# Attention on one core: TensorE's order written out by hand, and q's rotation moved from GpSimd to VectorE

## The chip, the cores and the metric

The kernel runs on one core of a Trainium2 chip. A core has five engines, each with an instruction queue of its own: TensorE (PE in the profile; its weight loads are listed apart as PEld), VectorE (DVE), ScalarE (ACT), GpSimd (POOL) and SyncE (SP). They wait for each other by semaphores; DMA transfers are started from such a queue, in this kernel mostly from SP's and POOL's. The metric is the device time of one execution in microseconds, as the median over several runs; lower is better. The profile is one execution of the program recorded by the hardware profiler.

## The reference

Two layers of a diffusion transformer on 256 tokens of width 2048, with 256 context tokens beside them, in float32. Layer 0 mixes by a Fourier transform; layer 1, where the change lies, is windowed attention with 64 query heads of width 64, which share 8 key and value heads, with a sink per head. Cut to what matters:

```python
def _attend_with_sink(q, k, v, sink, mask=None):
    s = jnp.einsum('bqhgd,bkhd->bhgqk', q, k).astype(jnp.float32) * (ATTN_HEAD_DIM ** -0.5)
    if mask is not None:
        s = jnp.where(mask, s, NEG_INF)
    sk = jnp.broadcast_to(sink.astype(jnp.float32)[None, :, :, None, None], s.shape[:-1] + (1,))
    p = jax.nn.softmax(jnp.concatenate([s, sk], axis=-1), axis=-1)[..., :-1]
    return jnp.einsum('bhgqk,bkhd->bqhgd', p.astype(v.dtype), v)

def _attention_branch(h, hc, w_in, sink, rows, cols, need_ctx):
    q, k, v, z = jnp.split(h @ w_in, [D_BRANCH, D_BRANCH + kvw, D_BRANCH + 2 * kvw], axis=-1)
    kc, vc = jnp.split(hc @ w_in[:, D_BRANCH:D_BRANCH + 2 * kvw], 2, axis=-1)
    ...
    q = _axial_rope(q.reshape(b, n, ATTN_Q_HEADS, ATTN_HEAD_DIM), rows, cols)
    k = _axial_rope(k.reshape(b, n, ATTN_KV_HEADS, ATTN_HEAD_DIM), rows, cols)
    ...
    o = lax.map(block, ...)
    y = jnp.moveaxis(o, 0, 1).reshape(b, n, D_BRANCH) * jax.nn.silu(z)
```

Behind it stands `x + gate * (y @ w_out[1])` and a last RMS norm. `_axial_rope` is the rotary step: the 64 features of each head are multiplied by a table of cosines, and their swapped quarters by a table of sines, and the two are added.

## The kernel before

All is one function, `tile_dit`, on a framework that takes the instructions in program order, orders those of each engine anew by a timeline that it estimates itself when the program is built, and sets the semaphores. The order on each engine is fixed from then on: an instruction that waits holds up all behind it on its engine. `tc.issue_after(ins)` adds an edge that keeps the instructions in its block behind `ins` on the same engine; it costs no instruction.

Precision: a float32 operand is split into a high and a low half (`split`, L65: a cast on ACT at L66, a subtraction on DVE at L67), and a product is three matmuls (`mm3`, L144: L145, L146, L147). `half_split` makes the two weight tiles (`wh`, `wl`) of 1024 columns for one unit; the pool has six such buffers, three units.

The attention stage interleaves two kinds of work on PE:

- *Filler units.* `units` (L1400) lists them in order: eight units for each group of 512 columns of q ("q", one group for each of the 8 key heads `hk`), two for each of the 32 blocks of the gate z ("z"), and 14 of the first part of the output projection ("o"). The list goes: q0, q1, four z blocks, q2, four z blocks, and so on; "o" units end it. `emit_unit` (L1434) emits the next one and prepares the weights of the one behind it. The last unit of a q group calls `finish_q` (L1359); the last of a z block makes the gate (L1474, L1475).
- *Pairs of heads.* There are 32 (`b`), four for each `hk`. `stage_s` (L1491) makes a pair's scores: 12 matmuls at L1504 into four PSUM banks; then masking and row minimum on DVE (L1507), the exponential on ACT (L1511), normalisation with a split into two float16 halves (L1526 on ACT, L1527 on DVE), and, for all but the last pair, four DMA transposes on SP's queue (L1529). `stage_o` (L1532) makes the value product of 24 matmuls at L1538 into one bank, and `emit_y` (L1481) multiplies it by the gate on DVE (L1487). Pair 31 is transposed on PE (`pe_turn`, L1394) just ahead of its value product.

The loop at L1562 emits for each `b`: scores of pair `b`, two filler units, the value product of pair `b - 1`, two filler units. Ten units are emitted before the loop (L1543). What PE really does in which order is the framework's choice.

`finish_q` takes a finished q group from its two PSUM banks (`oq`, one for each block of 128 tokens). For `hk` 0, ACT takes the sum of squares (L1365) and DVE makes the rotary step straight from PSUM. For the other seven, ACT copies the bank to SBUF (L1369), takes the sum of squares (L1370), and POOL makes the rotary step from the copy. `roped` (L1129) is the step: one multiplication of 512 columns (L1132), two of 256 (L1137) and one addition of 512 (L1138), on the engine that it is given; without one it is DVE. Then four small operations on DVE turn the sum of squares into a scale (L1376 to L1379), and the scaling and split into float16 (`q_parts`: L1387 on ACT, L1388 on DVE) are deferred by some slots; the result `qt` is transposed on PE for `hk` 0 (L1397, with copies at L1398) and by DMA on SP's queue for the others (L1390). `prep_kk` (L1348) splits the keys of the group on ACT (L1354) and POOL (L1356).

PSUM has 8 banks, all of one pool: four for a pair's scores, one for a value product, two for a q group, one for a z block.

Of the kernel before, what the change touches and what calls it, by code (L numbers as in the profile page):

```python
# [13 lines left out]
AF = mybir.ActivationFunctionType  # L14
# [3 lines left out]
P = 128  # L18
D = 2048
KT = D // P  # L20
DB = 4096
NB = DB // P
N = 256
# [9 lines left out]
def tile_dit(ctx: ExitStack, tc: tile.TileContext, a: dict, out: bass.AP):  # L33
    nc = tc.nc
    V, S, PE, GP = nc.vector, nc.scalar, nc.tensor, nc.gpsimd
# [4 lines left out]
    actp = ctx.enter_context(tc.tile_pool(name="act", bufs=33))  # L40
# [14 lines left out]
    def act(dt=F32):  # L55
        return actp.tile([P, 512], dt, tag="act", name="act")
# [87 lines left out]
    def mm3(o, wh, wl, xh, xl, start, stop):  # L144
        PE.matmul(o, wh, xh, start=start, stop=False)  # L145
        PE.matmul(o, wh, xl, start=False, stop=False)  # L146
        return PE.matmul(o, wl, xh, start=False, stop=stop).ins  # L147
# [491 lines left out]
    for g in range(G):  # L639
        for j in {13: (8, 9), 14: (10, 11)}.get(g, (g - 5,) if 5 <= g < 13 else ()):  # L640
            t = up.tile([P, 1024], F32, name="pz", tag="pz", bufs=1)
# [13 lines left out]
        if g == 3:  # L655
            with tc.issue_after(f0_end[0]):
                f3 = [fold_uh(load_uh(g, kh), g, kh) for kh in range(2)]
            w = [split_uh(*f3[0]), {"m": split_part("m", f3[1][1])}]
# [3 lines left out]
        elif g == 4:  # L662
            w = []
# [476 lines left out]
    with tc.tile_pool(name="h1", reuse_waits="tile", bufs=16) as h1p:  # L1140
# [130 lines left out]
        with tc.tile_pool(name="at", reuse_waits="tile", bufs=2) as at:  # L1271
# [55 lines left out]
            def o1_step(k, os_, wh, wl):  # L1327
                while len(yh) <= min(k + 4, NB - 1) and (len(yh) < 28 or fin):
                    y_split(len(yh))
                for tb in range(2):  # L1330
                    mm3(os_[tb], yh[k][:, tb * P : (tb + 1) * P], yh[k][:, N + tb * P : N + (tb + 1) * P], wh, wl, k == 0, k == NB - 1)
            slot = [0]

            def k_turn(hp):
# [24 lines left out]
            def finish_q(hk, oq):  # L1359
                sq = at.tile([P, 2, 4], F32, tag="sq", name="sq")  # L1360
                qr = []
                for tb in range(2):
                    t = act()
                    if hk == 0:
                        S.activation(act(), oq[tb], AF.Square, accum_out=sq[:, tb, 0:1])  # L1365
                        roped(t, oq[tb], tb, actp, "act")
                    else:
                        t0 = act()
                        S.copy(t0, oq[tb])  # L1369
                        S.activation(act(), oq[tb], AF.Square, accum_out=sq[:, tb, 0:1])  # L1370
                        roped(t, t0, tb, actp, "act", GP)
                    qr.append(t)
                if hk:
                    prep_kk(hk)
                x, up, sc = (sq[:, :, c] for c in (1, 2, 3))
                V.tensor_scalar(x, sq[:, :, 0], 2.0**-70, None, op0=ALU.max)  # L1376
                V.tensor_scalar(x.bitcast(I32), x.bitcast(I32), 24, 23, op0=ALU.logical_shift_right, op1=ALU.logical_shift_left)
                V.tensor_scalar(up.bitcast(I32), x.bitcast(I32), -1.0, 204.0 * 2**23, op0=ALU.mult, op1=ALU.add)
                V.tensor_scalar(sc.bitcast(I32), x.bitcast(I32), kx.bitcast(I32), -30.0 * 2**23 - 2.0**31, op0=ALU.add, op1=ALU.add)  # L1379
                qt = at.tile([P, 8, 2, P], F16, tag="qt", name="qt")  # L1380
                qq[hk] = qt, sc
                for tb in range(2):
                    defer.append((slot[0], lambda tb=tb: q_parts(hk, tb, qt, qr[tb], up[:, tb : tb + 1])))
# [10 lines left out]
            def pe_turn(ft, f, tb):  # L1394
                o = pp.tile([P, 8, P], F16, tag="ps", name="ps")
                for j in range(8):
                    PE.transpose(o[:, j, :], f[:, j * P : (j + 1) * P], ident16)  # L1397
                (S.copy if tb == 0 else V.tensor_copy)(ft[:, :, tb, :], o)  # L1398
# [31 lines left out]
                return half_split(raws1[src], i % 2)  # L1430

            ready = {}

            def emit_unit():  # L1434
                if pos[0] >= len(ulist):
                    return
                u = ulist[pos[0]]
                if pos[0] not in ready:
                    ready[pos[0]] = prep(u)
                if pos[0] + 1 < len(ulist):  # L1440
                    ready[pos[0] + 1] = prep(ulist[pos[0] + 1])
                w = ready.pop(pos[0])
                pos[0] += 1
                kind, n, i, o = u
                if kind == "o":
                    if n == 0:
                        oA.extend([psum(), psum()])
                    for j in range(2):
                        o1_step(n * 2 + j, oA, *(t[:, j * 512 : (j + 1) * 512] for t in w))
                    return  # L1450
                wh, wl = w
                if kind == "q":
                    if i == 0:
                        o += [psum(), psum()]
                    if (n, i) == (0, 4):
                        with tc.issue_after(last_cast[0]):
                            prep_kk(0)
                    for j in range(2):
                        k = i * 2 + j
                        q = slice(j * 512, (j + 1) * 512)  # L1460
                        for tb in range(2):
                            mm3(o[tb], hx1[k][:, tb * P : (tb + 1) * P], hx1[k][:, N + tb * P : N + (tb + 1) * P], wh[:, q], wl[:, q], k == 0, k == KT - 1)
                    if i == 7:
                        finish_q(n, o)
                else:
                    if i == 0:
                        o.append(psum())
                    for k in range(i * 8, i * 8 + 8):
                        q = slice((k % 8) * P, (k % 8 + 1) * P)
                        mm3(o[0][:, 0:N], wh[:, q], wl[:, q], hx1[k][:, 0:N], hx1[k][:, N : 2 * N], k == 0, k == KT - 1)  # L1470
                    if i == 1:
                        th = at.tile([P, N], F32, tag="th", name="th", bufs=3)
                        zs = o[0][:, 0:N]
                        S.activation(th, zs, AF.Tanh, scale=0.5)  # L1474
                        V.scalar_tensor_tensor(th, th, 1.0, zs, op0=ALU.add, op1=ALU.mult)  # L1475
                        szs[n] = th
                        emit_y(n)
# [13 lines left out]
            def stage_s(b):  # L1491
# [6 lines left out]
                for tb in range(2):  # L1498
                    for hh in range(2):
                        so[hh, tb] = psum()  # L1500
                    for n, (jj, kx_) in enumerate(((j, kkh), (4 + j, kkh), (j, kkl))):
                        for hh in range(2):
                            r = slice(hh * 64, hh * 64 + 64)
                            PE.matmul(so[hh, tb], qt[r, jj, tb, :], kx_[r, :], start=n == 0, stop=n == 2)  # L1504
                    for hh in range(2):
                        o = so[hh, tb]
                        V.tensor_tensor_reduce(o, o, mask[:, tb, :], sc[:, tb : tb + 1], nsink[:, 2 * b + hh : 2 * b + hh + 1], ALU.add, ALU.min, mx[:, hh, tb : tb + 1])  # L1507
# [24 lines left out]
            def stage_o(blk, pair):  # L1532
                hk = blk // 4
                oo = psum()[:, 0:N]
                steps = [(kb, c, j) for kb in range(4) for c, j in ((0, kb), (64, kb), (0, 4 + kb))]
                for n, (kb, c, j) in enumerate(steps):
                    for hh, ft in enumerate(pair):
                        PE.matmul(oo[hh * 64 : hh * 64 + 64, :], v01[kb][:, hk, c : c + 64], ft[:, j, :, :].rearrange("p t q -> p (t q)"), start=n == 0, stop=n == len(steps) - 1)  # L1538
                obs[blk, 1] = oo
                emit_y(blk)  # L1540

# [9 lines left out]
            while defer:  # L1551
                defer.pop(0)[1]()

            def filler():
                j = slot[0]
                slot[0] += 1
                emit_unit()
                if defer and defer[0][0] + 2 < j:
                    defer.pop(0)[1]()

            pts = {}
            for b in range(33):  # L1562
                if b % 4 == 0:
                    while defer:
                        defer.pop(0)[1]()
                y_sums(12, 2 * b if b < 30 else 99)
                if b == 31:
                    out_scale()
                if b < 32:
                    pts[b] = stage_s(b)  # L1570
                filler()
                filler()
                if b:
                    ft, fs = pts.pop(b - 1)
                    for (hh, tb), f in fs.items():
                        pe_turn(ft[hh], f, tb)
                    stage_o(b - 1, ft)
                filler()
                filler()


        with tc.tile_pool(name="fin", reuse_waits="tile", bufs=1) as fp:
# [243 lines left out]
```

## Time and profile before

| | us |
|---|---|
| median of three runs | 1780.81 (1779.39 to 1782.48) |
| the profiled execution | 1778.66 |
| its span, first to last instruction | 1776.9 |
| PE busy in the span | 1717.7 |
| DVE busy in the span | 1385.8 |
| ACT busy in the span | 1112.8 |
| POOL busy in the span | 342.2 |

The attention stage's pairs run from about 1132 us (first scores) to 1637 us (last value product) of the span. A row of an order-of-time view gives start and length in microseconds, engine, line, operation, what is written from what, shapes and how many instructions the row merges; in square brackets stands the idle time of the engine just before it and what ended it. A row of the waits gives engine, tile and line that waited, what for, the total in microseconds, how often, and the longest. A matmul's recorded length overlaps that of the next; the distance between starts is what it costs. PE is counted busy by these overlapping lengths.

### The profile page before, as it was taken

What the parts mean: (1) busy time and instruction counts of PE and PEld (TensorE: products, weight loads), DVE (VectorE), ACT (ScalarE), POOL (GpSimd) and SP (SyncE); (2) the same over time, 40 slices, a digit from 0 to 9 for tenths busy, and PEclk for the clock granted to TensorE, in tenths of its full rate; (3) what the DMA queues carried; (4) which work ended last, traced back from release to release, by engine and by line L of the source; (5) the groups of instructions that cost most, each with busy time, mean ns of one, the idle gap of its engine ahead of it and who ended that gap; (6) DMA issues with size and microseconds to landing.
All of it is one profiled execution on the core that took longest, in us unless ns stands there. A gap on an engine that the chain in (4) does not pass through costs nothing. (4 is left out here: it accounts for less than half of the span.)

```text
span 1776.9 us, 28302 instructions
## 1 busy us (share of the span) xinstructions
PE 1717.7 (97%) x10379; PEld 1134.2 (64%) x10379; DVE 1385.8 (78%) x2334; ACT 1112.8 (63%) x2125; POOL 342.2 (19%) x485
## 2 busy tenths in 40 slices
PE   6999999999999999999999999699999999999998
PEld 4679999544444444446445646588777777877464
DVE  5779888797777796877687786878888889887755
ACT  5545556477768745465235696666677777786643
POOL 0002111212222115112311122202202220251001
PEclk9999999999999999999999999899999999999999
DMA  9998998778998969976997692588798788888643
GB/s 394 417 354 254 277 274 244 301 286 315 327 308 313 318 224 368 357 285 261 378 339 222 213 351 104 166 199 197 211 243 207 201 223 231 201 209 289 222 177 119
DMA packets 249196, 469.95 MB, mean 264 GB/s; under 512 B 171392, under 2 KB 171792, under 8 KB 222176
## 3 DMA queue, kind: packets, MB, share of 16 engines
q1 hardware_dynamic: 197568, 335.60, 57.9%
q0 software_dynamic: 47344, 125.58, 22.2%
q10 hardware_dynamic: 4144, 6.95, 1.1%
q8 instruction: 81, 1.33, 0.3%
q14 instruction: 59, 0.48, 0.1%
HBM read 419.30 MB, written 12.59 MB: 243 GB/s over the span
## 5 line engine op out<-in xcount | busy, mean ns | idle before, releaser
L67 DVE TENSOR_TENSOR wl<-raw,wh 128x1024 fp32r<-128x1024 f32 x152 | 191.5, 1270 | 101.8 <-ACT wh L66 85.8
L66 ACT CAST wh<-raw 128x1024 fp32r<-128x1024 f32 x152 | 158.1, 1046 | 81.7 <-PE ps L146 61.8
L146 PE MATMUL ps<-act,wf 128*128 128x512 f16 x512 | 194.0, 379 | 0.0
L147 PE MATMUL ps<-act,wf 128*128 128x512 f16 x512 | 191.1, 379 | 0.0
L145 PE MATMUL ps<-act,wf 128*128 128x512 f16 x512 | 189.8, 379 | 0.6 <-ACT wf L137 0.2
L145 PE MATMUL ps<-y,wf 128*128 128x512 f16 x448 | 169.8, 379 | 0.8 <-ACT wf L137 0.8
L146 PE MATMUL ps<-y,wf 128*128 128x512 f16 x448 | 169.8, 379 | 0.0
L147 PEld LDWEIGHTS <-wf 128*128 128x128 f16 x960 | 93.9, 98 | 113.1
L145 PEld LDWEIGHTS <-wf 128*128 128x128 f16 x960 | 93.7, 98 | 113.2 <-ACT wf L137 4.2
L147 PE MATMUL ps<-y,wf 128*128 128x512 f16 x448 | 164.9, 379 | 0.0
L146 PEld LDWEIGHTS <-wf 128*128 128x128 f16 x960 | 93.9, 98 | 109.1
L147 PE MATMUL ps<-h,wl 128*128 128x256 f32 x512 | 144.6, 282 | 6.3 <-DVE wl L67 6.2
L145 PE MATMUL ps<-h,wh 128*128 128x256 f32 x512 | 147.4, 288 | 0.0
L137 ACT ACTIVATE wf<-raw,nrm 128x1024 f16<-128x1024 f32 x56 | 63.5, 1146 | 131.9 <-PE ps L147 71.2
L1511 ACT ACTIVATE p<-ps,mx 128x512 f32<-128x512 f32 x128 | 87.8, 687 | 89.1 <-DVE mx L1507 84.9
L146 PE MATMUL ps<-h,wh 128*128 128x256 f32 x512 | 143.6, 280 | 0.0
L138 DVE SCALAR_TENSOR_TENSOR wf<-raw,tn,wf 128x1024 f16<-128x1024 f32 x64 | 79.8, 1282 | 42.7 <-ACT wf L137 42.6
L829 ACT ACTIVATE act<-act 128x512 f32<-128x512 f32 x178 | 109.5, 617 | 5.0 <-DMA act<-in_wo 4.5
L790 POOL DMA_DIRECT2D wa<-in_adw x64 | 34.2, 535 | 370.6 <-PE ps L147 143.1
L1527 DVE SCALAR_TENSOR_TENSOR f<-p,sm,f 128x512 f16<-128x512 f32 x128 | 104.5, 870 | 1.4 <-ACT f L1526 1.4
L145 PEld LDWEIGHTS ps<-h,wh 128*128 128x128 f32 x512 | 96.8, 189 | 10.0 <-ACT th L1474 4.2
L145 PE MATMUL ps<-wh,h 128*128 128x512 f32 x256 | 102.8, 407 | 0.0
(436 smaller groups left out, 4799.8 us busy)
## 6 DMA issues: line engine op xcount, KB each, us to landing
raw<-in_wz SPq DMA_DIRECT2D x64, 1024.0 KB, 5.3
raw<-in_awp SPq DMA_DIRECT2D x32, 1024.0 KB, 12.7
zr<-in_adw SPq DMA_DIRECT2D x64, 512.0 KB, 6.9
wa<-in_adw POOLq DMA_DIRECT2D x64, 512.0 KB, 6.6
act<-in_wo POOLq DMA_DIRECT2D x128, 256.0 KB, 7.2
raw<-in_wo SPq DMA_DIRECT2D x32, 1024.0 KB, 8.4
raw<-in_wq SPq DMA_DIRECT2D x32, 1024.0 KB, 5.4
raw<-in_wu SPq DMA_DIRECT2D x32, 1016.0 KB, 7.0
```

The costliest lines, as they stand in the source:

```text
L66: last_cast[0] = S.copy(h, src).ins
L67: last_sub[0] = eng.tensor_tensor(l, src, h.bitcast(F32), op=ALU.subtract).ins
L137: last_cast[0] = S.activation(w[:, 0], src, AF.Copy, scale=up).ins
L138: last_sub[0] = V.scalar_tensor_tensor(w[:, 1], src, up, w[:, 0], op0=ALU.mult, op1=ALU.subtract).ins
L145: PE.matmul(o, wh, xh, start=start, stop=False)
L146: PE.matmul(o, wh, xl, start=False, stop=False)
L147: return PE.matmul(o, wl, xh, start=False, stop=stop).ins
L790: nc.gpsimd.dma_start(wf, a["adw"][i, kh, fg][:, q])
L829: S.activation(t, t, AF.Square, accum_out=c)
L1511: S.activation(pt[hh, tb], so[hh, tb], AF.Exp, bias=mx[:, hh, tb : tb + 1], scale=-1.0, accum_out=sm[:, hh, tb : tb + 1])
L1527: f_last[:] = fa, V.scalar_tensor_tensor(f[:, 512:1024], pt[hh, tb], s1, f[:, 0:512], op0=ALU.mult, op1=ALU.subtract).ins
```

## The change

The loop emits four filler units at once between a pair's scores and the value product of the preceding pair, in place of two and two, and each piece's matmuls are put behind the last matmul of the piece before it by `issue_after`, so that PE's order in the loop is the one written down: scores of pair `b`, four units, value product of pair `b - 1`. In the last turn, which has no scores, three units come ahead of the value product and one behind it. The ten units before the loop are not ordered in this way among themselves; the first scores come behind the last of them. `pe_last` carries the last matmul from piece to piece.

In `finish_q`, all eight groups now do what `hk` 0 did: ACT takes the sum of squares from PSUM, DVE makes the rotary step straight from PSUM, and the copy on ACT and POOL's rotary step are gone.

```diff
@@ o1_step
                 for tb in range(2):
-                    mm3(os_[tb], ..., wh, wl, k == 0, k == NB - 1)
+                    r = mm3(os_[tb], ..., wh, wl, k == 0, k == NB - 1)
+                return r
@@ finish_q
                 for tb in range(2):
                     t = act()
-                    if hk == 0:
-                        S.activation(act(), oq[tb], AF.Square, accum_out=sq[:, tb, 0:1])
-                        roped(t, oq[tb], tb, actp, "act")
-                    else:
-                        t0 = act()
-                        S.copy(t0, oq[tb])
-                        S.activation(act(), oq[tb], AF.Square, accum_out=sq[:, tb, 0:1])
-                        roped(t, t0, tb, actp, "act", GP)
+                    S.activation(act(), oq[tb], AF.Square, accum_out=sq[:, tb, 0:1])
+                    roped(t, oq[tb], tb, actp, "act")
                     qr.append(t)
@@ emit_unit, stage_s and stage_o: each keeps its last matmul in pe_last, as here
-                            mm3(o[tb], hx1[k]..., wh[:, q], wl[:, q], k == 0, k == KT - 1)
+                            pe_last[0] = mm3(o[tb], hx1[k]..., wh[:, q], wl[:, q], k == 0, k == KT - 1)
@@ the loop
-            def filler():
-                j = slot[0]
-                slot[0] += 1
-                emit_unit()
-                if defer and defer[0][0] + 2 < j:
-                    defer.pop(0)[1]()
+            def filler(n):
+                for _ in range(n):
+                    j = slot[0]
+                    slot[0] += 1
+                    with tc.issue_after(pe_last[0]):
+                        emit_unit()
+                    if defer and defer[0][0] + 2 < j:
+                        defer.pop(0)[1]()
...
                 if b < 32:
-                    pts[b] = stage_s(b)
-                filler()
-                filler()
+                    with tc.issue_after(pe_last[0]):
+                        pts[b] = stage_s(b)
+                filler(4 if b < 32 else 3)
                 if b:
                     ft, fs = pts.pop(b - 1)
-                    for (hh, tb), f in fs.items():
-                        pe_turn(ft[hh], f, tb)
-                    stage_o(b - 1, ft)
-                filler()
-                filler()
+                    with tc.issue_after(pe_last[0]):
+                        for (hh, tb), f in fs.items():
+                            pe_turn(ft[hh], f, tb)
+                        stage_o(b - 1, ft)
+                if b == 32:
+                    filler(1)
```

More of the change, by code (lines that the diff above doesn't have):

```diff
@@ L1330, in o1_step @@
                 for tb in range(2):
-                    mm3(os_[tb], yh[k][:, tb * P : (tb + 1) * P], yh[k][:, N + tb * P : N + (tb + 1) * P], wh, wl, k == 0, k == NB - 1)
+                    r = mm3(os_[tb], yh[k][:, tb * P : (tb + 1) * P], yh[k][:, N + tb * P : N + (tb + 1) * P], wh, wl, k == 0, k == NB - 1)
+                return r
             slot = [0]
@@ L1432, in tile_dit @@
             ready = {}
+            pe_last = [None]
             def emit_unit():
@@ L1448, in emit_unit @@
                     for j in range(2):
-                        o1_step(n * 2 + j, oA, *(t[:, j * 512 : (j + 1) * 512] for t in w))
+                        pe_last[0] = o1_step(n * 2 + j, oA, *(t[:, j * 512 : (j + 1) * 512] for t in w))
                     return
@@ L1461, in emit_unit @@
                         for tb in range(2):
-                            mm3(o[tb], hx1[k][:, tb * P : (tb + 1) * P], hx1[k][:, N + tb * P : N + (tb + 1) * P], wh[:, q], wl[:, q], k == 0, k == KT - 1)
+                            pe_last[0] = mm3(o[tb], hx1[k][:, tb * P : (tb + 1) * P], hx1[k][:, N + tb * P : N + (tb + 1) * P], wh[:, q], wl[:, q], k == 0, k == KT - 1)
                     if i == 7:
@@ L1469, in emit_unit @@
                         q = slice((k % 8) * P, (k % 8 + 1) * P)
-                        mm3(o[0][:, 0:N], wh[:, q], wl[:, q], hx1[k][:, 0:N], hx1[k][:, N : 2 * N], k == 0, k == KT - 1)
+                        pe_last[0] = mm3(o[0][:, 0:N], wh[:, q], wl[:, q], hx1[k][:, 0:N], hx1[k][:, N : 2 * N], k == 0, k == KT - 1)
                     if i == 1:
@@ L1503, in stage_s @@
                             r = slice(hh * 64, hh * 64 + 64)
-                            PE.matmul(so[hh, tb], qt[r, jj, tb, :], kx_[r, :], start=n == 0, stop=n == 2)
+                            pe_last[0] = PE.matmul(so[hh, tb], qt[r, jj, tb, :], kx_[r, :], start=n == 0, stop=n == 2).ins
                     for hh in range(2):
@@ L1537, in stage_o @@
                     for hh, ft in enumerate(pair):
-                        PE.matmul(oo[hh * 64 : hh * 64 + 64, :], v01[kb][:, hk, c : c + 64], ft[:, j, :, :].rearrange("p t q -> p (t q)"), start=n == 0, stop=n == len(steps) - 1)
+                        pe_last[0] = PE.matmul(oo[hh * 64 : hh * 64 + 64, :], v01[kb][:, hk, c : c + 64], ft[:, j, :, :].rearrange("p t q -> p (t q)"), start=n == 0, stop=n == len(steps) - 1).ins
                 obs[blk, 1] = oo
```

## The prediction

> **What bounds the kernel now.** I read the page first, then the stretches of the attention stage, then TensorE's own waits there, and last the order of single instructions around the longest wait.
>
> ```profile
> span 1776.9 us, 28302 instructions
> PE 1717.7 (97%) x10379; PEld 1134.2 (64%) x10379; DVE 1385.8 (78%) x2334; ACT 1112.8 (63%) x2125; POOL 342.2 (19%) x485
> ```
> ```profile
> 1138.00:1158.00 20.00, 5.38 (x36) 4.79 (x34) 15.33 (x25) 12.63 (x29) 9.55 (x8) 0.66 0.55 95
> 1158.00:1570.00 412.00, 398.58 (x3013) 327.92 (x3008) 350.54 (x582) 302.99 (x603) 71.66 (x60) 1.00 0.86 215
> 1570.00:1640.00 70.00, 67.23 (x431) 49.86 (x430) 56.21 (x91) 54.53 (x105) 28.76 (x34) 1.00 0.87 258
> 1640.00:1777.00 137.00, 127.97 (x592) 72.13 (x589) 82.86 (x91) 63.28 (x77) 13.97 (x10) 0.98 0.47 169
> ```
>
> (The columns of the stretches: length, busy time of PE, its weight loads, DVE, ACT and POOL, granted clock, DMA share, GB/s.) PE is the bound: 97% of the span. What a change of order can win is only the time in which PE stands still: 20.00 - 5.38 = 14.6 us in the first stretch, 412.00 - 398.58 = 13.4 us in the second, 2.8 us in the third. PE is full behind that until its last few microseconds, so a microsecond won in attention should reach the end. PE's waits after the first stretch, grouped (window 1160 to 1640), are these:
>
> ```profile
> PE ps L1538 <- DMA ft<-f: 7.1, 12, 1.0
> PE ps L147 <- DVE wl L67: 6.2, 7, 1.0
> PE ps L146 <- DVE wl L67: 2.8, 1, 2.8
> ```
>
> The value product (L1538) waits 7.1 us in all for transposed probabilities, filler matmuls 6.2 us and once 2.8 us for low weight halves that DVE makes. The large wait, in order of time:
>
> ```profile
> 1134.13 0.38 PE L1504 MATMUL ps<-kkl,qt 64*128 64x512 f16 x2
> ...
> 1137.87 0.39 PE L1504 MATMUL ps<-kkl,qt 64*128 64x512 f16 x2
> 1152.88 0.39 PE L1538 MATMUL ps<-ft,v 128*64 128x256 f16 x1 [14.62 <-ACT f L1526]
> 1153.21 0.58 PE L145 MATMUL ps<-h,wh 128*128 128x256 f32 x1
> ...
> 1156.56 0.28 PE L145 MATMUL ps<-h,wh 128*128 128x256 f32 x1
> 1156.68 0.28 PE L146 MATMUL ps<-h,wh 128*128 128x256 f32 x1
> ```
>
> Pair 0's scores end at 1134.5, pair 1's come soon after, and then its value product was put ahead of the z units: PE stands 14.62 us. Behind the wait the granted clock is low (0.66 in that stretch): 15 matmuls take 1156.56 - 1153.21 = 3.35 us where the later spacing of 0.12 gives 1.8, so 1.6 us more is lost.
>
> **The change, part by part. 1. That wait goes.** In the new order pair 0's value product follows its scores by 8 filler units and the scores of pair 1. What they last:
>
> ```profile
> 1236.94 0.60 PE L1504 MATMUL ps<-kkh,qt 64*128 64x512 f16 x4
> ...
> 1245.29 1.50 PE L1538 MATMUL ps<-ft,v 128*64 128x256 f16 x23 [0.80 <-DMA ft<-f]
> 1246.71 0.50 PE L145 MATMUL ps<-wh,h 128*128 128x512 f32 x1
> ...
> 1252.50 0.61 PE L1504 MATMUL ps<-kkh,qt 64*128 64x512 f16 x4
> ```
>
> Two units of q last 1252.50 - 1246.71 = 5.8 us: 2.9 us a unit. Scores and value product take 1.4 us each, as first to last start shows. So 8 x 2.9 + 1.4 = 24.6 us stand where the chain of softmax and transposes took 1152.88 - 1134.51 = 18.4 us. The wait and its slow clock go: **-16.2 us**.
>
> **2. A new wait takes part of it back.** In before the scheduler pulled q1's units ahead of pair 0's scores while the first q was being rotated. Now only units 8 and 9 may stand there; unit 10 is behind the scores. The chain from q0's last matmul:
>
> ```profile
> 1111.25 0.60 ACT L1365 ACTIVATE act<-ps 128x512 f32<-128x512 f32 x1 [1.18 <-PE ps L147]
> 1112.71 0.68 DVE L1132 TENSOR_TENSOR act<-ps,rope 128x512 f32<-128x512 f32 x1
> 1113.31 0.74 DVE L1137 TENSOR_TENSOR rt<-ps,rope 128x256 f32<-128x256 f32 x2
> 1115.11 0.68 DVE L1138 TENSOR_TENSOR act<-act,rt 128x512 f32<-128x512 f32 x1
> 1119.98 0.16 DVE L1378 TENSOR_SCALAR sq<-sq 128x2 int32<-128x2 int32 x1
> 1121.07 1.33 ACT L1387 ACTIVATE fq<-act,sq 128x512 f16<-128x512 f32 x2
> 1122.34 1.41 DVE L1388 SCALAR_TENSOR_TENSOR fq<-act,sq,fq 128x512 f16<-128x512 f32 x2
> 1126.21 1.07 PE L1397 MATMUL ps<-ident,fq 128*128 128x128 f16 x16
> 1127.99 0.68 DVE L1398 COPY qt<-ps 128x1024 f16<-128x1024 f16 x1
> 1132.39 0.61 PE L1504 MATMUL ps<-kkh,qt 64*128 64x512 f16 x4
> ```
>
> q0 ends at 1111.15; units 8 and 9 fill 5.8 us, to 1116.9. The scale is there at 1120.1 (L1378). ACT's fq came at 1121.07 behind a weight cast of a unit that now can't be due, so I let it start at 1120.1; with the halves of fq overlapped (0.7 us each), the turn of the second half (0.5) and the copy (0.7), the scores start near 1123.1. Of 1123.1 - 1116.9 = 6.2 us the turn itself is 1.07 us of work that before had too: **+5.1 us** of waiting. Behind the waiting scores stand all further units on PE; ACT and DVE run out of weight buffers to fill until these run, so nothing else is done meanwhile. From below: if DVE puts its weight subtractions behind the rotation, 3 us less, some 2 us. From above: qt ready as late as in before, at 1128.7, less the turn, 10.8 us. I take the value between because its steps are the rows.
>
> A low clock behind the new wait: the nearest rows are the 14.62 us wait (1.6 us lost) and this 2.77 us one, behind which the spacing is the usual 0.24:
>
> ```profile
> 1595.05 0.50 PE L146 MATMUL ps<-wl,ys 128*128 128x512 f32 x1 [2.77 <-DVE wl L67]
> 1595.38 0.39 PE L147 MATMUL ps<-wh,ys 128*128 128x512 f32 x1
> 1595.62 0.39 PE L146 MATMUL ps<-wl,ys 128*128 128x512 f32 x1
> ```
>
> 5.1 lies nearer to 2.77: 0 in the sum, 1.6 us in the range. [...]
>
> **3. The steady turn.** From scores to scores nothing moves but the value product: by two units, 5.8 us, later. Its waits were at most 1.0 us each; all 7.1 us should go: **-7.1 us**, bounds 0 and 7.1. It issues no DMA, so SP's queue keeps its order against the scores. The move costs nothing else: the probabilities' buffers hold two pairs, and the freed PSUM bank and the gate product behind it (L1487) are needed only a turn or more later.
>
> **4. The rotation on DVE.** In one period (16 units, four pairs; 7 such rotations):
>
> ```profile
> 1213.50 1.29 POOL L1132 TENSOR_TENSOR act<-act,rope 128x512 f32<-128x512 f32 x1 [32.24 <-issue]
> 1219.77 2.97 POOL L1138 TENSOR_TENSOR act<-act,rt 128x512 f32<-128x512 f32 x2
> ```
> ```profile
> 1216.49 0.70 DVE L1376 TENSOR_SCALAR sq<-sq 128x2 f32<-128x2 f32 x1
> 1217.22 1.22 DVE L1377 TENSOR_SCALAR sq<-sq 128x2 int32<-128x2 int32 x1
> 1219.74 4.87 DVE L1527 SCALAR_TENSOR_TENSOR f<-p,sm,f 128x512 f16<-128x512 f32 x4
> 1224.54 2.35 DVE L67 TENSOR_TENSOR wl<-raw,wh 128x1024 fp32r<-128x1024 f32 x2
> 1236.15 2.74 DVE L1527 SCALAR_TENSOR_TENSOR f<-p,sm,f 128x512 f16<-128x512 f32 x4
> ```
>
> DVE gains 2 x (0.68 + 0.74 + 0.68) = 4.2 us a period, 29 us in seven. But while POOL rotates (1213.5 to 1222.7), DVE's four f take 4.87 us against 2.74 after it, and L1376 and L1377 take 0.70 and 1.22 against the 0.16 of L1378 without POOL: 2.1 + 1.6 = 3.7 us given back, with more on L1378, L1379 and the weight subtraction. DVE's load is about even. The subtraction at 1224.54 is the one that filler matmuls wait for (1.0 us a period); without POOL it should come no later, by my count up to 2 us sooner. Bounds: 6.2 us gained, 7 lost (the wait doubled); I take **-4 us**, as most of it hangs on one instruction that moves forward. ACT loses 14 copies from PSUM and POOL its rotation; neither bounds PE.
>
> [...]
>
> **5. The end.** The four turns of pair 31 now stand directly ahead of its value product, no filler among them: one copy (0.7 to 1.0 us, L1398) shows: **+1 us**, 0 to 2. The 2.77 us wait stays (0 to -2.8).
>
> **The sum.** -16.2 + 5.1 - 7.1 - 4 + 1 = -21.2 us. The profiled execution took 1778.66 us, 1.8 us around its span of 1776.9; that gives 1757.5. It lies 2.15 us below the median of 1780.81, so the median to come is 1757.5 + 2.15 = **1759.6 us**. Ends of the terms: -16.2 + 2 - 7.1 - 6.2 - 2.8 = -30.3 (1750.5); with half of part 3, nothing from part 4 and the dear ends of the rest, -16.2 + 10.8 + 1.6 - 3.6 + 2 = -5.4 (1775.4).
>
> **Rivals.** *The late start eats the gain*: the first q's chain isn't shortened (10.8 + 1.6 us) and the small waits only halve (-3.6, -2): -16.2 + 12.4 - 5.6 + 1 = -8.4, about 1772. For it: PE has nothing but two units there. Against: half of the chain's slack in the rows is queueing behind units that move away.
>
> *DVE becomes the bound, slower*: DVE is busy 350.54 of 412 us (85%). If the rotation is queued in front of the weight subtraction and POOL's absence gives nothing, PE waits the whole 4.2 us a period, also for the PSUM banks of q, which now stay occupied until DVE is through: 7 x 4.2 = 29 us, against -16.2 + 5.1 - 7.1 + 1 = -17.2: 1793. It decides from 17.2 / 7 = 2.5 us a period. For it: seven waits on that subtraction already. Against: the giveback of 3.7 us.
>
> *It does little*: the fixed order moves the wait without shortening it, because the scheduler lays the other engines' queues anew around it; new waits of 0.6 us at each of 32 pairs cost 19 us: 1779.
>
> **How the numbers follow.** Forecast 0.60 (1751 to 1768), late start 0.20 (1768 to 1776), little 0.09, DVE as the bound 0.11. The range 1751 to 1776 holds the first two, 0.80, and the ends of the terms. What a measurement here can tell from no change is about 0.2%, 3.6 us: faster 0.80, same 0.09, slower 0.11.
>
> **What will show it.** No value product of pair 0 waiting over 1 us; a wait of 2 to 11 us ahead of the first scores; L1538 without waits on the transposes; L1527 near 0.7 us after a rotation; L1132 on DVE 16 times in attention near 0.68. I am wrong if waits on wl grow beyond 6.2 us, or if scores wait for PSUM.

## The result, and the profile after

The changed kernel takes **1752.2 us** (median of 4 runs, 1751.69 to 1753.47) against 1780.1 us, a ratio of 0.984 with a 95% interval of 0.983 to 0.986: 28 us faster. The forecast was 1759.6 us, 21 us faster, in a range of 1751 to 1776. The time lies inside the range, near its low end, so two things have to be explained: that it became faster, and where 7 us more than the sum came from. Terms of the sum were wrong in both directions. One of the four runs of the kernel with both rotations, below, took 2905 us at a granted clock of 0.56; it is a slow run and is left out of that kernel's median.

The page after, lines of the span and of the engines:

```profile
span 1749.9 us, 28309 instructions
PE 1708.5 (98%) x10379; PEld 1131.3 (65%) x10379; DVE 1376.4 (79%) x2390; ACT 1103.4 (63%) x2111; POOL 281.2 (16%) x429
```

PE makes the same 10379 matmuls in 27.0 us less span. DVE, which took over seven rotations, is busy 9 us *less* than before, and POOL 61 us less. PE's waits in the attention stage after (window 1100 to 1620), in the columns of before:

```profile
PE ps L1534 <- ACT ft L1393: 6.9, 1, 6.9
PE ps L1392 <- ACT fq L1382: 3.4, 1, 3.4
PE ps L146 <- DVE wl L67: 1.8, 2, 0.9
PE ps L1500 <- ACT qt L1393: 0.7, 1, 0.7
```

The lines have moved by four or five: L1500 is the scores (L1504 before), L1534 the value product (L1538), L1392 the turn on PE (L1397), a transpose, not to be mixed up with a turn of the loop. The 14.62 us wait, the twelve waits for transposes and the seven on L147 are gone. Two new ones stand there: 3.4 + 0.7 us ahead of the first scores, which was forecast, and 6.9 us ahead of the last value product, which was priced at 1.

To see where the time went, one point of each trace is enough: the first matmul of a pair's scores. Rows of pair 2 and pair 29 before, then after, in order of time:

```profile
1162.16 0.61 PE L1504 MATMUL ps<-kkh,qt 64*128 64x512 f16 x4
...
1572.57 0.61 PE L1504 MATMUL ps<-kkh,qt 64*128 64x512 f16 x4
```
```profile
1153.30 0.61 PE L1500 MATMUL ps<-kkh,qt 64*128 64x512 f16 x4
...
1537.90 0.61 PE L1500 MATMUL ps<-kkh,qt 64*128 64x512 f16 x4
```

They cut the span into three. Up to pair 2: 8.9 us won. The 27 turns of the loop between: 410.4 us before, 384.6 after, 25.8 us won. From pair 29 to the end: 1776.9 - 1572.57 = 204.3 before, 1749.9 - 1537.90 = 212.0 after, 7.7 us lost. The sum is 27.0 us, that of the spans. The sum on record had -11.1, -11.1 and +1 in the same three places.

PE's order of time after, around the new wait ahead of the first scores:

```profile
1117.83 0.39 PE L147 MATMUL ps<-wh,h 128*128 128x512 f32 x1
1121.66 2.07 PE L1392 MATMUL ps<-ident,fq 128*128 128x128 f16 x16 [3.44 <-ACT fq L1382]
1124.41 1.04 PE L1500 MATMUL ps<-kkh,qt 64*128 64x512 f16 x4 [0.68 <-ACT qt L1393]
...
1127.09 0.80 PE L145 MATMUL ps<-wh,h 128*128 128x512 f32 x1
1127.68 0.63 PE L146 MATMUL ps<-wl,h 128*128 128x512 f32 x1
1128.11 0.49 PE L147 MATMUL ps<-wh,h 128*128 128x512 f32 x1
```

Idle are 4.1 us. But behind the 3.44 us everything is slow, at a granted clock of 0.51 from 1121.6 to 1128.4 and 1.00 in the 4.6 us after that: the same 16 turns last 2.07 us instead of 1.07, the scores take 2.7 us from start to start (1124.41 to 1127.09) instead of 1.4, and the first filler matmuls are 0.59 and 0.43 apart instead of 0.23. That is 1.0 + 1.3 + 0.6 = 2.9 us on top, of which 0.3 us is a second wait: between the two halves of the turns PE's weight loads stand 0.27 us for ACT's second fq.

And around the wait ahead of the last value product, PE first, then ACT, then DVE:

```profile
1592.74 1.96 PE L1392 MATMUL ps<-ident,f 128*128 128x128 f16 x32
1601.61 0.37 PE L1534 MATMUL ps<-ft,v 128*64 128x256 f16 x1 [6.90 <-ACT ft L1393]
```
```profile
1597.86 2.19 ACT L137 ACTIVATE wf<-raw,adab 128x1024 f16<-128x1024 f32 x2 [5.16 <-DMA raw<-in_wo1b]
1599.95 0.70 ACT L1312 ACTIVATE yf<-act,adab 128x512 f16<-128x512 f32 x1
1600.57 1.90 ACT L1393 COPY ft<-ps 128x1024 f16<-128x1024 f16 x2
```
```profile
1599.04 1.28 DVE L138 SCALAR_TENSOR_TENSOR wf<-raw,adab,wf 128x1024 f16<-128x1024 f32 x1 [4.81 <-ACT wf L137]
1600.24 1.28 DVE L1393 COPY ft<-ps 128x1024 f16<-128x1024 f16 x2
```

PE's turns are done at 1594.7. The copies that they need stand on ACT and on DVE behind weight casts of the *next* stage (L137, L138), and these wait for a weight load. Both engines took them in that order (ACT's cast at 1597.86, its copies at 1600.57; DVE's at 1599.04 and 1600.24), so PE waits for a load that its value product doesn't use. The profile names only the last link ("ACT ft"); the cause stands two rows further up, on the queue of the engine named.

### The profile page after: what moved, and what is told of

Its sections match the earlier page's. It is cut to its first block, busy times and chain, and to the rows that moved or that the text cites. A ratio compares the mean times of both kernels' runs of the same rounds, so it can differ in the third digit from the quotient of the medians.

```text
span 1749.9 us, 28309 instructions
## 1 busy us (share of the span) xinstructions
PE 1708.5 (98%) x10379; PEld 1131.3 (65%) x10379; DVE 1376.4 (79%) x2390; ACT 1103.4 (63%) x2111; POOL 281.2 (16%) x429
## 5 line engine op out<-in xcount | busy, mean ns | idle before, releaser
L67 DVE TENSOR_TENSOR wl<-raw,wh 128x1024 fp32r<-128x1024 f32 x152 | 189.7, 1262 | 50.1 <-ACT wh L66 41.9
L147 PE MATMUL ps<-act,wf 128*128 128x512 f16 x512 | 191.1, 379 | 0.0
L147 PEld LDWEIGHTS <-wf 128*128 128x128 f16 x960 | 93.9, 98 | 113.1
L147 PE MATMUL ps<-y,wf 128*128 128x512 f16 x448 | 164.9, 379 | 0.0
L137 ACT ACTIVATE wf<-raw,nrm 128x1024 f16<-128x1024 f32 x56 | 63.5, 1145 | 132.6 <-PE ps L147 73.7
L145 PE MATMUL ps<-h,wh 128*128 128x256 f32 x512 | 144.3, 282 | 0.0
L147 PE MATMUL ps<-h,wl 128*128 128x256 f32 x512 | 142.6, 279 | 0.1
L146 PE MATMUL ps<-h,wh 128*128 128x256 f32 x512 | 142.7, 279 | 0.0
L138 DVE SCALAR_TENSOR_TENSOR wf<-raw,tn,wf 128x1024 f16<-128x1024 f32 x64 | 79.8, 1281 | 42.6 <-ACT wf L137 42.6
L146 PE MATMUL ps<-wl,h 128*128 128x512 f32 x256 | 101.6, 397 | 0.0
L147 PE MATMUL ps<-wh,h 128*128 128x512 f32 x256 | 101.2, 395 | 0.0
L145 PE MATMUL ps<-wh,h 128*128 128x512 f32 x256 | 100.4, 403 | 0.0
```

Of the source, the lines that this page charges most:

```text
L67: last_sub[0] = eng.tensor_tensor(l, src, h.bitcast(F32), op=ALU.subtract).ins
L137: last_cast[0] = S.activation(w[:, 0], src, AF.Copy, scale=up).ins
L138: last_sub[0] = V.scalar_tensor_tensor(w[:, 1], src, up, w[:, 0], op0=ALU.mult, op1=ALU.subtract).ins
```

## The experiments

Theory after the result: the fixed order removes the long wait and the waits of the value product, and taking the rotation off GpSimd frees DVE and removes the waits on weight halves. Its rivals: only one of the two parts matters; the rotation is a load on DVE; the pinning counts, not the place of the value product. Each kernel below is timed against the kernel before in the same runs (1779.9 to 1781.2 us there). "27 turns" and "rest" are worked out as above, from the first start of the scores of pairs 2 and 29 and the span's end in each trace. A trace is one execution, and its time can lie off the median of its kernel: by 3.5 us for order only (1770.8), by some 2 or less for the others. With 12 units ahead of the first scores, two units (5.7 us) more stand ahead of pair 2 and two fewer behind pair 29, so the last two rows have these 5.7 us in another column.

| kernel | median us | ratio, 95% interval | pair 2 starts | 27 turns | rest |
|---|---|---|---|---|---|
| before | 1780.1 | | 1162.2 | 410.4 | 204.3 |
| changed | 1752.2 | 0.984 (0.983 to 0.986) | 1153.3 | 384.6 | 212.0 |
| order only | 1767.3 | 0.993 (0.991 to 0.994) | 1152.2 | 406.3 | 210.5 |
| rotation only | 1763.9 | 0.990 (0.988 to 0.992) | 1162.7 | 393.1 | 204.3 |
| both rotations | 1763.9 | 0.990 (0.988 to 0.993) | 1152.9 | 397.9 | 212.3 |
| copies only | 1750.7 | 0.984 (0.982 to 0.986) | 1151.7 | 384.9 | 211.7 |
| memsets | 1751.3 | 0.984 (0.983 to 0.986) | 1152.5 | 385.8 | 210.9 |
| two and two | 1754.8 | 0.985 (0.983 to 0.987) | 1151.8 | 392.3 | 207.1 |
| three and one | 1756.9 | 0.986 (0.985 to 0.988) | 1153.4 | 391.1 | 212.2 |
| turns earlier | 1741.7 | 0.978 (0.977 to 0.979) | 1152.8 | 385.4 | 201.7 |
| 12 units first | 1744.4 | 0.979 (0.978 to 0.981) | 1152.4 | 384.5 | 206.3 |
| both of these | 1736.0 | 0.975 (0.973 to 0.976) | 1152.3 | 384.5 | 197.4 |

**1. Order only.** The changed kernel with `finish_q` as before.

```diff
-                    S.activation(act(), oq[tb], AF.Square, accum_out=sq[:, tb, 0:1])
-                    roped(t, oq[tb], tb, actp, "act")
+                    if hk == 0:
+                        S.activation(act(), oq[tb], AF.Square, accum_out=sq[:, tb, 0:1])
+                        roped(t, oq[tb], tb, actp, "act")
+                    else:
+                        t0 = act()
+                        S.copy(t0, oq[tb])
+                        S.activation(act(), oq[tb], AF.Square, accum_out=sq[:, tb, 0:1])
+                        roped(t, t0, tb, actp, "act", GP)
```

> PE's order as in the changed kernel, the rotation of q1 to q7 back on GpSimd with its ACT copy. My theory: the long wait and the waits of the value product stay away, but DVE is slowed again while GpSimd rotates, so the 1.0 us waits of filler matmuls on weight halves come back (seven or eight, 7.6 us by the distances between starts in before): 1757 to 1764 us. Rival 1, the rotation's place is of no account: 1750 to 1754. Rival 2, the rotation is a load on DVE that costs time: 1742 to 1748.

1767.3 us: dearer than the theory had it. The long wait is gone and the turns' waits for transposes too, but the 27 turns take 406.3 us, hardly less than before (in an execution 3.5 us slower than the median). PE's waits, window 1170 to 1535:

```profile
PE ps L145 <- ACT wh L66: 5.6, 6, 1.7
PE ps L147 <- DVE wl L67: 4.5, 6, 0.8
PE ps L146 <- DVE wl L67: 0.6, 2, 0.4
```

Beside DVE's low halves PE now waits for ACT's high halves, which no row of PE's waits in before shows. ACT in order of time, behind one q group:

```profile
1276.92 0.72 ACT L1388 ACTIVATE fq<-act,sq 128x512 f16<-128x512 f32 x1 [3.89 <-POOL act L1138]
1279.16 0.72 ACT L1388 ACTIVATE fq<-act,sq 128x512 f16<-128x512 f32 x1 [1.51 <-POOL act L1138]
```

In this schedule the scaling of q stands so early in ACT's queue that it waits 3.89 and 1.51 us for POOL's slow addition (4.58 us for the two; one takes 0.68 on DVE in the changed kernel), with the weight casts behind it; all 14 scalings of q1 to q7 wait so, 31.6 us in all. So the rotation on POOL costs through two queues, DVE's and ACT's.

**2. Rotation only.** The kernel before with the changed `finish_q`.

> The rotation on DVE, PE's order left to the framework. My theory: the long wait ahead of pair 0's value product stays, some 3 us shorter at most, the 1.0 us waits on weight halves go (7.6 us): 1767 to 1773 us; waits of the value product on transposes stay or halve. Rival, the fixed order does nothing beyond the rotation: 1752. Rival, DVE's load costs: above 1780.

1763.9 us, 3 us below the theory's range: 17 us from the rotation alone, more than the order alone gives (14). The long wait stays (13.9 us). But the waits for transposes go almost as well: 27 turns in 393.1 us, and PE's waits are, from 1130 to 1640,

```profile
PE ps L1532 <- DMA ft<-f: 14.9, 3, 13.9
PE ps L146 <- DVE wl L67: 2.8, 1, 2.8
```

Of the 14.9 us one wait is 13.9, so 1.0 us is left in all other pairs, with the value product still only two units behind the scores. So step 3 of the prediction has only half of it: the later place takes these waits away (order only, where POOL still rotates), but a chain that POOL does not slow takes most of them away as well, with the value product where it was.

**3. Both rotations, and its two controls.** The changed kernel, in which POOL does the old rotation as well, from a copy, into a tile that nothing reads:

```diff
                     roped(t, oq[tb], tb, actp, "act")
+                    if hk:
+                        t0 = act()
+                        S.copy(t0, oq[tb])
+                        roped(act(), t0, tb, actp, "act", GP)
```

> The changed kernel, with GpSimd's copy and rotation done as well into tiles that nothing reads (for q1 to q7), so DVE does as much as in the changed kernel but beside a busy GpSimd. If GpSimd's sharing with DVE is what cost DVE its time in before: the probabilities' split takes about 1.2 instead of 0.68 us during it, waits on weight halves return and grow, 1760 to 1775 us. If not: 1751 to 1755 us, the split at 0.68.

1763.9 us: 12 us lost with the same work on DVE. The theory's time holds; its sign on the probabilities' split doesn't, since in this schedule the split is over (0.68 us each, 2.73 for four) before POOL begins. Others are hit, and filler matmuls wait for low halves again. PE's waits, window 1170 to 1535:

```profile
PE ps L147 <- DVE wl L67: 7.4, 7, 1.2
PE ps L146 <- DVE wl L67: 0.9, 3, 0.3
```

DVE, then POOL, in order of time:

```profile
1271.21 0.68 DVE L1132 TENSOR_TENSOR act<-ps,rope 128x512 f32<-128x512 f32 x1
...
1272.47 0.68 DVE L1375 TENSOR_SCALAR sq<-sq 128x2 f32<-128x2 f32 x1
...
1274.53 0.90 DVE L1138 TENSOR_TENSOR act<-act,rt 128x512 f32<-128x512 f32 x1
1275.35 1.25 DVE L1376 TENSOR_SCALAR sq<-sq 128x2 int32<-128x2 int32 x1
```
```profile
1269.17 3.26 POOL L1132 TENSOR_TENSOR act<-act,rope 128x512 f32<-128x512 f32 x1 [34.51 <-issue]
1272.39 2.49 POOL L1137 TENSOR_TENSOR rt<-act,rope 128x256 f32<-128x256 f32 x2
1274.96 1.62 POOL L1138 TENSOR_TENSOR act<-act,rt 128x512 f32<-128x512 f32 x1
```

While POOL works, operations on two columns take 0.68 and 1.25 us, which take 0.16 without it. The multiplication out of PSUM keeps its 0.68. POOL suffers as well: its first multiplication takes 3.26 us instead of 1.29.

The first control does the copies alone (`S.copy(act(), oq[tb])`), the second gives POOL nine memsets in place of each copy and rotation:

```diff
+                    if hk:
+                        t0 = act()
+                        for _ in range(9):
+                            GP.memset(t0, 0.0)
```

> The changed kernel with the old ACT copies of q1 to q7 done as well, into tiles that nothing reads, and no rotation on GpSimd: the control for the kernel with both rotations. If GpSimd's rotation cost the 12 us there, 1751 to 1754 us here; if ACT's copies did, 1760 to 1766.

> The changed kernel with GpSimd busy for about as long as a rotation took (18 memsets of a 128x512 tile a group, some 0.5 us each, for q1 to q7), writing SBUF and reading none, no copy on ACT. If any work on GpSimd slows DVE: waits on weight halves come back, 1758 to 1766 us. If it is the reading of two SBUF operands that does it: 1751 to 1755 us, the probabilities' split at 0.75 us.

1750.7 and 1751.3 us: neither costs anything. The copies are cleared. The memsets need a reservation: the framework put them behind POOL's key split, some 20 us later in the period than DVE's rotation (1286.22 against 1262.48 to 1268.6), so the time alone says little. What can be read there is DVE's durations beside them:

```profile
1172.36 8.96 POOL L1370 MEMSET act<- 128x512 f32 x18
```
```profile
1176.11 1.23 DVE L67 TENSOR_TENSOR wl<-raw,wh 128x1024 fp32r<-128x1024 f32 x1 [0.29 <-ACT wh L66]
...
1177.59 2.73 DVE L1527 SCALAR_TENSOR_TENSOR f<-p,sm,f 128x512 f16<-128x512 f32 x4
```

Four splits in 2.73 us with POOL writing the whole time, against 4.87 us beside the rotation in before. So a busy POOL alone did not slow these splits: its memsets, which read nothing, left them as they are, and its rotation, which reads two operands from SBUF, stretched them. So did its subtraction at L67, with two operands as well: beside it the four splits take 4.18 us in the changed kernel (at 1550.35).

**4. Two and two, three and one.** The changed kernel with the value product pinned at another place; the edit is that of two and two, three and one has `filler(3)` and `filler(1)`.

```diff
-                filler(4 if b < 32 else 3)
+                filler(2)
                 if b:
...
-                if b == 32:
-                    filler(1)
+                filler(2)
```

> The changed kernel with two units, value product, two units, all pinned in that order. My theory: pair 0's value product follows its scores by six units and one score, 18.8 us, about what the chain takes, so the long wait is mostly gone; a part of the waits on transposes returns (0 to 10 us) and there is one switch more between kinds of work in a turn, 0.2 us each, some 6 us: 1758 to 1768 us. Rival, that the order is pinned is all that counts, not where the value product stands: 1750 to 1754.

> The changed kernel with three units, value product, one unit, pinned. The value product still follows its scores by seven units, 23 us, so by my theory its waits stay away; what is added is one switch between kinds of work in a turn. By the distances between starts it costs 0.2 us: 31 turns, 6 us: 1756 to 1760 us. Rival, switches are free and only waits count: 1750 to 1754.

1754.8 and 1756.9 us. Two and two beats the theory's 1758 to 1768; its trace has one wait of 0.6 us for transposes in the turns. With the rotation gone from POOL, the place of the value product matters little for waiting. Yet the 27 turns take 392.3 and 391.1 us against 384.6. Three and one has no wait of PE at all in them (window 1170 to 1535), so its 6.5 us, 0.24 us a turn, are the price of one more switch between kinds of matmul: with four units at once, value product and next scores follow each other. Cutting the 27 turns into their pieces, each from its first start to the next piece's first start, shows it:

| us in 27 turns | scores | value products | filler units |
|---|---|---|---|
| before | 37.8 | 47.5 | 325.1 |
| order only | 37.8 | 39.2 | 329.4 |
| rotation only | 37.8 | 40.7 | 314.7 |
| two and two | 37.8 | 39.9 | 314.7 |
| three and one | 37.8 | 38.6 | 314.7 |
| both rotations | 37.8 | 38.7 | 321.4 |
| changed | 37.8 | 38.7 | 308.1 |

Three kernels with two stretches of filler units in a turn and no wait in them have 314.7 us, the changed kernel with one stretch has 308.1: 6.5 us for the switch. Before has 10.4 us above 314.7 in its filler units and 8.9 us above 38.6 in its value products. Of the 10.4, 1.8 us are two waits ahead of a value product's first matmul, which this cut puts to the piece before. So the value products' waits cost 10.7 us, those on weight halves 8.6 and the switch 6.5: together the 25.8 us won. The switch is what only the fixed order gains in the steady turn; the value products' waits go with either part, those on weight halves only with the rotation. (In the whole time two and two is near the changed kernel because its rest is 5 us shorter: its last value product waits 1.7 us, not 6.9.)

**5. The two new waits.** Pair 31's turns two units earlier; 12 units ahead of the first scores; both.

```diff
-                filler(4 if b < 32 else 3)
+                if b < 32:
+                    filler(4)
+                else:
+                    filler(1)
+                    with tc.issue_after(pe_last[0]):
+                        for (hh, tb), f in pts[31][1].items():
+                            pe_turn(pts[31][0][hh], f, tb)
+                    filler(2)
...
-                        for (hh, tb), f in fs.items():
-                            pe_turn(ft[hh], f, tb)
```
```diff
-                        th = at.tile([P, N], F32, tag="th", name="th", bufs=3)
+                        th = at.tile([P, N], F32, tag="th", name="th", bufs=4)
...
-            first = 10
+            first = 12
```

With both, the last turn has two units left: one ahead of the turns of pair 31 and one behind them.

> The changed kernel, with the four turns of pair 31 behind the first filler unit of the last turn instead of the third. My theory: the 6.9 us wait ahead of the last value product is there because the copies of the turns stand on ACT and DVE behind weight casts that wait for a weight load; two units earlier they stand ahead of them, and the wait goes with its slow clock (2 us): 1742 to 1746 us. Rival, the weight load is late for PE too and the wait only moves behind the value product: 1750 to 1753.

> The changed kernel, with 12 instead of 10 units ahead of the first scores (and one more buffer for the gate; the last turn has two units less). My theory: the waits ahead of the first scores go (3.44 and 0.68 us), and the slow clock behind them too (3 us by the doubled distances): 1744 to 1747 us. If the slow clock had another cause: 1747 to 1750. Rival, the two units are missed at the end and the wait there grows by as much: 1751 to 1754.

> 12 units ahead of the first scores, and the turns of pair 31 behind the first of the last two units. If the two gains add: 1734 to 1739 us. If the units are missed at the end: 1740 to 1746.

1741.7, 1744.4 and 1736.0 us: the first just under its theory's range, the other two inside. The first shows that the last wait was the order of ACT's and DVE's queues and not the weight load itself: with the copies ahead of the casts the rest takes 201.7 us instead of 212.0, and PE doesn't wait for the load elsewhere. With 12 units the wait ahead of the scores shrinks to 0.77 us and the scores run at speed (PE in order of time):

```profile
1123.41 1.25 PE L1392 MATMUL ps<-ident,fq 128*128 128x128 f16 x16
1125.43 0.60 PE L1500 MATMUL ps<-kkh,qt 64*128 64x512 f16 x4 [0.77 <-ACT qt L1393]
...
1127.13 0.50 PE L145 MATMUL ps<-wh,h 128*128 128x512 f32 x1
```

1.7 us from the first score to the first filler matmul instead of 2.7. Of the gain of 7.8 us, 4.1 - 0.8 us of idle time and the 2.9 us behind it account for 6.2; by the traces the gain is 6.7 us (spans of 1749.9 and 1743.2), so most of the other 1.6 lies between these traces and the medians. The two don't quite add (10.6 and 7.8, together 16.2): with both, the rest is 1.4 us longer than with the earlier turns alone (197.4 + 5.7 against 201.7). **1736.0 us is the fastest version found**: 0.975 of the time before.

## Why the prediction was right, and where it was wrong

**Right: what bounds, and the long wait (step 1).** PE was the bound, and the 14.62 us wait was a matter of order: it stays with the rotation alone (13.9 us) and is gone in every kernel with a pinned order. (The chain was counted from the end of rows that hold half of pair 1's scores too; pair 0's twelve end at 1133.7, so it took 19.2 us and not 18.4, still less than 24.6.) The signs named ahead came: no wait of pair 0's value product, 4.1 us ahead of the first scores, no wait for transposes or PSUM, DVE's split at 0.75 us on average and 16 rotary multiplications on it at 0.68.

**In part luck: the range.** The turns won 25.8 us where 11.1 were forecast; the head gave 2.2 us less than forecast and the end cost 6.7 us more. Errors of opposite sign left the span 5.8 us under the sum. The other 1.6 us below the forecast come from the trace after lying 0.5 us under its median, where 2.15 had been added.

**Right, but undersized: the new wait (step 2, +5.1).** The scores came where the rows put them: 1124.41 less the 0.7 us by which the chain began later (1111.96 against 1111.25) is 1123.7, against 1123.1 forecast. The 5.1 us turned out as 3.4 + 0.7 us of idle time and 1.0 us of longer turns. What failed is the choice on the clock: 5.1 us was held to be nearer to a 2.77 us wait without slow matmuls than to the 14.62 us one, and 0 was taken. Slow matmuls behind it cost 1.3 us in the scores and 0.6 in the first filler matmuls; these 1.9 us came on top of the 5.1 and are more than the 1.6 that the range allowed, for the turn and the scores ran in the slow time too. Waits shorter than 5.1 us had it too: behind those of 3.06 and 3.04 us (two and two, three and one) matmuls ran 0.43 and 0.42 us apart instead of 0.24. With the measured cost, idle and on top, the first part of the span, -16.2 + 4.1 + 2.9 = -9.2, comes near the traces: 8.9 us by pair 2's start, or 9.6 counted from the sum of squares of q0, the chain's first step, which began 0.7 us later after.

**Near in size, half of the cause: the waits of the value product (step 3, -7.1).** They cost 10.7 us in the turns and went. As the step says, two units more are enough: with the order alone they are gone while POOL still rotates (39.2 us of value products against 47.5). But so is the rotation's move: with it alone 2.0 us are left by the starts (40.7 against 38.7), the value product only two units behind the scores. The rotation on POOL had slowed DVE's part of the chain ahead of the transposes. The prediction held the row that says so (four splits in 4.87 us) and used it only for the weight halves; it counted as independent two terms that take away the same wait.

**Wrong in size: the rotation (step 4, -4).** It was called even for DVE's load and worth 4 us. Alone it gives 17 us, all of it in the 27 turns (410.4 to 393.1): 8.6 us of waits on weight halves and 8.7 of the value product's. Three things were missed. The waits of step 3 go with it too. All waits on weight halves in the turns went, not most. And idle time understates a wait: the idle column counts from the recorded end of a matmul that overlaps the next. By the distance of starts, the six waits written as 1.0 us cost 1.15 us more than the usual spacing each (1.27 against 0.12), and the value product's twelve waits some 9.5 us against 7.1 (10.6 us from start to start, less what the usual spacing gives).

**Missed: the switch.** Step 3 said that nothing moves but the value product, and that the move costs nothing else. One switch between kinds of matmul less in a turn moves too: 6.5 us in 27 turns by the three-and-one kernel, a term that the sum did not have. The rows for it were there (starts around scores and value products in before), unused.

**Wrong in size: the end (step 5, +1).** It counted the copy's duration and not its place in ACT's and DVE's queues. The wait was 6.9 us, and 2 us of slow clock stand behind it: 22 matmuls take 1608.85 - 1601.91 = 6.9 us, which at 0.22 apart are 4.8; the granted clock was 0.69 from 1601.6 to 1608.9 and 1.00 in the 4.1 us after that. From pair 29 on 7.7 us were lost, where 1 was forecast; the 2.77 us wait on a low half became two of 0.9.

**The rivals.** The late start did not come (4.1 us of idle time, not 10.8), nor did new waits in the turns (PE has none between 1170 and 1535), nor DVE as the bound: DVE's busy time fell, and the kernel with POOL's rotation on top shows that the giveback, not the added load, decides.

## What to carry to other kernels

Before moving an operation off an engine, look at the durations of the *other* engines' instructions while it runs: the rotation was off PE's path, and still it was worth 17 us of 1780, because it stretched what DVE did beside it (four splits from 2.74 to 4.87 us). When an order is pinned, walk the waiting instruction's inputs back to the queue that makes each of them, and see what stands ahead of them there; both new waits were visible in the code, and undoing them gained 16 us more. And price a wait by the distance of starts, with the slow matmuls behind it (2.9 us on top of 4.1 idle ahead of the first scores), not by the idle column.

## What the runs showed of the hardware

The clock: behind the wait of 2.77 us (before) the spacing is 0.24 as usual, at a granted clock of 1.00 from 1595 to 1600. Behind one of 3.06 us (two and two) matmuls are 0.43 apart for 2.7 us, and behind the 3.44 us one (changed), with 1.0 us more of waiting among them, everything runs slow for 6.7 us, at a granted clock of 0.51. PE in order of time, two and two, then three and one:

```profile
1566.57 0.79 PE L146 MATMUL ps<-wl,ys 128*128 128x512 f32 x1 [3.06 <-DVE wl L67]
1567.16 0.63 PE L147 MATMUL ps<-wh,ys 128*128 128x512 f32 x1
1567.59 0.63 PE L146 MATMUL ps<-wl,ys 128*128 128x512 f32 x1
```
```profile
1566.93 0.50 PE L146 MATMUL ps<-wl,ys 128*128 128x512 f32 x1 [3.04 <-DVE wl L67]
1567.26 0.40 PE L147 MATMUL ps<-wh,ys 128*128 128x512 f32 x1
...
1568.52 0.63 PE L147 MATMUL ps<-wh,ys 128*128 128x512 f32 x1
1568.94 0.63 PE L145 MATMUL ps<-wh,ys 128*128 128x512 f32 x1
```

In three and one the second matmul behind the wait still lasts 0.40 us, as in before, and those at 1568.52 and 1568.94 last 0.63 and start 0.42 apart: the slow time need not begin where the wait ends. By the spacing, the wait of 3.06 us cost 1.3 us on top of itself, the one of 2.77 us nothing; where the edge lies, and what sets the moment, these runs don't settle.

DVE beside GpSimd: the smallest operations suffered most, 0.16 to 1.25 us for two columns. In the kernel with both rotations two of the stretched ones of the group shown end 0.02 and 0.03 us behind an instruction of POOL (1276.60 against 1276.58, 1280.65 against 1280.62); why, no view shows. Operations out of PSUM kept their times beside the rotation there (0.68 us at L1132, 0.74 for two at L1137), and beside POOL's memsets four splits took 2.73 us, a subtraction at L67 1.23 and an operation on four columns 0.16, all as without them. Of the operations with two SBUF inputs, four splits took 4.87 us beside the rotation in before against 2.74 behind it, and a subtraction 1.64 against 1.23; but beside the rotation in the kernel with both, one subtraction took 1.21 us (at 1273.06). Which inputs on DVE's side decide is not shown. That it depends on what POOL does is what the splits show: 4.87 us beside its rotation, 2.73 beside its memsets.
